# MLP and FFN activations turned by VectorE and through DRAM instead of by TensorE

## The chip, the cores and the metric

One core of one Trainium2 chip. The metric is the device time of one execution in microseconds (us), as a median of several. The core's engines are TensorE (PE; its weight loads are listed apart as PEld), VectorE (DVE), ScalarE (ACT), GpSimd (POOL) and SyncE (SP). Each runs its own instructions in order; they wait for each other by semaphores. Memory transfers are issued by an engine and carried out by 16 DMA engines.

## The reference

256 tokens of width 1024 pass through two blocks in float32. The first has four layers, each a mixer and a squared-ReLU MLP; the second has two layers, each an FFN, a token mixer, another FFN and a gated product:

```
h = squared_relu_mlp(rms_norm(x, g), w1, w2)      # square(relu(x @ w1)) @ w2, 1024 -> 4096 -> 1024
x = x + rms_norm(h, g)
...
x = layer_norm(a * x + 0.5 * (silu(x @ w1) * (x @ w3)) @ w2)      # 1024 -> 2816 -> 1024
x = layer_norm(a * x + token_mixing(x))
x = layer_norm(a * x + 0.5 * swiglu(x))
x = layer_norm(a * x + sigmoid(x @ w_gate) * (p @ w_proj))
```

So there are four MLPs and four FFNs. In both, the inner activations (after relu and square, or after silu and product) are the left operand of the second matrix.

## The kernel before

**Halves and units.** The tokens are cut into two halves of 128 (half 0 and half 1), one Python generator each. A unit is a piece of weights of 128 x 1024. `drive` hands the units out in the order of a plan: half 0 takes a unit, half 1 the same unit some units later (`PACE`: 4 units in these stages). A half's work on one unit is six matmuls of 512 columns, since products are made in three parts (`mm3`): the left operand is split into a rounded high part `t2h` and the rest `t2l`, the weights into `wh` and `whl`; high by high, high by low and low by high are summed.

**Weights.** SP loads a unit into a raw buffer (`raw`, `rawx`: 3 + 2 of them). ScalarE casts it to `wh` or `whx`, VectorE subtracts to get `whl` or `whxl` (`split_unit`). There are 4 + 4 of these pairs. A raw buffer is free again after the subtraction, a pair after half 1's matmuls. In steady running half 1 ends unit v-8 while half 0 works on v-4, so the cast of unit v can begin when half 0 starts unit v-3.

**MLP and FFN.** An MLP has 8 groups of 512 inner columns, an FFN 11 of 256. For group g a half does the first product (`w1(g)`: 4 units) into a PSUM bank `mm`, makes the inner tile (`relu2`, 128x512, or `glu`, 128x256; tokens are the partitions), and later multiplies it by the second matrix (4 or 2 units) into `acc`. For that product the inner index has to lie on the partitions: `tr` turns the tile on TensorE in 128x128 pieces (four or two) into a PSUM bank `tp`, and `split` takes `t2h` and `t2l` from there by ScalarE and VectorE. The order in a half is `w1(0)`, `w1(1)`, product 0, `w1(2)`, product 1, and so on; the last product comes without a first product ahead of it. Product g's second unit is where the split of tile g+1 is asked for.

After an MLP or FFN, a chain on VectorE and GpSimd makes the new `x`, and `x` (or `xn`) is turned on TensorE for the next stage.

**Order.** The program is recorded in this order, and a scheduler then sets each engine's own order by a model of times, so matmuls of the two halves and of neighbouring stages interleave. Small tiles come from two rings (`s1` up to 264 columns, `s2`) whose buffer numbers stand in `RINGS`.

Of the kernel before, what the change touches and what calls it, by code (L numbers as in the profile page):

```python
# [10 lines left out]
F32 = mybir.dt.float32  # L11
# [4 lines left out]
ALU = mybir.AluOpType  # L16
# [8 lines left out]
EXTRA = {"1": (2, 4), "A": (2, 4), "M": (0, 2)}  # L25

RM = (42, 20)
RINGS = {"1": (30, 6), "A": (20, 6), "M": RM}
SIDE_1 = 1.6
H_L = 8.0  # L30
H_P = 9.0
# [19 lines left out]
class Builder:  # L51
    def __init__(s, ctx, tc, io):
        s.ctx, s.tc, s.nc, s.io = ctx, tc, tc.nc, io
        s.pin = tc.keep_in_program_order
        s.kind = None
        eng = s.nc.tensor
        m0, t0 = eng.matmul, eng.transpose
        def mmp(out, a, b, **k):
            r = m0(out, a, b, **k)  # L59
            n = math.prod(b.shape[1:])  # L60
            K = b.shape[0]
            f = b.dtype == F32R
            s.clock += (0.000417 * n if f else 0.001668 * max(n, 0.96 * math.prod(a.shape[1:])) * (0.75 if K == 64 else 0.6 if K == 32 else 1))
            return s.pin(r) if s.kind in PINK else r
        def trp(*a, **k):
            r = t0(*a, **k)  # L66
            s.clock += 0.107
            return s.pin(r) if s.kind in PINK else r
        s.clock = 0.0
        eng.matmul, eng.transpose = mmp, trp  # L70
        pool = lambda name, bufs, **k: ctx.enter_context(tc.tile_pool(name=name, bufs=bufs, **k))
        s.const = pool("const", 1)
        s.raw = pool("raw", RAWP)
        s.wsp = pool("wsp", WHP)
        s.vec = pool("vec", 4)
        s.st = pool("st", 8)
        s.ps = pool("ps", 1, space=PSUM)
        s.turn = False
        s.stack = None
        s.plan, s.width, s.segs = [], {}, []  # L80
        s.rawq, s.whq = ["raw"] * RAWP, ["wh"] * WHP
        s.slot, s.r, s.w, s.sh = {}, {}, {}, {}
        s.loaded = s.split_to = 0
        s.loaded_par = None
        s.pin_ = {}
        s.spaced = False
        s.splits = 0
        s.first_cast = s.first_rin = None
        nc = s.nc
        s.ident = s.const.tile([128, 128], F32, name="ident")  # L90
        make_identity(nc, s.ident)
        s.nhalf = s.const.tile([128, 1], F32, name="nhalf")
        nc.vector.memset(s.nhalf, -0.5)


    def phase(s, kind, what):
# [4 lines left out]
        s.pool = s.stack.enter_context(s.tc.tile_pool(name=f"ph{len(s.slot)}", bufs=1))  # L101
        s.rings = RINGS[kind]
        s.spaced = False
# [236 lines left out]
    def split(s, src):  # L340
        nc = s.nc
        n = src.shape[1]
        hh = s.B2((128, n, 128), "t2h", F32R)
        ll = s.B2((128, n, 128), "t2l", F32R)
        a = nc.scalar.copy(hh, src)  # L345
        b = nc.vector.tensor_tensor(ll, src, hh.bitcast(F32), op=ALU.subtract)  # L346
        if s.splits < 2:
            s.first_split = a.ins, b.ins
        s.splits += 1
        return hh, ll  # L350

    def tr(s, src, n=4):
        tp = s.tpb()
        for j in range(n):
            s.nc.tensor.transpose(tp[:, j, :], src[:, j * 128:(j + 1) * 128], s.ident)
        return tp

    def tr_split(s, src):
        return s.split(s.tr(src))
# [84 lines left out]
    def mlp(s, h, lhs, rin):  # L444
        nc = s.nc
        out = [s.acc(), s.acc()]
        r = {}

        def w1(g):
            mm = s.mmb()  # L450
            for k in range(0, 8, 2):
                W = yield "w1"
                for kk in range(2):
                    s.mm3(lhs, k + kk, W, [(mm, kk * 512, 512, k + kk == 0, k + kk == 7)])
            a = s.B2(name="relu")
            nc.scalar.activation(a, mm, AF.Relu, scale=rin)
            a2 = s.B2(name="relu2")
            nc.vector.tensor_tensor(a2, a, a, op=ALU.mult)
            r[g] = a2

        yield from w1(0)
        for g in range(8):
            if g < 7:
                yield from w1(g + 1)
            at = nxt if g else [s.tr_split(r.pop(g))]
            for k in range(4):
                W = yield "w2"
                if g < 7 and k == 1:
                    nxt = [s.tr_split(r.pop(g + 1))]
                s.mm3(at, k, W, [(out[c], c * 512, 512, g == 0 and k == 0, g == 7 and k == 3) for c in range(2)])  # L470
        return out

# [368 lines left out]
    def ffn(s, h, lhs):  # L841
        nc = s.nc
        out = [s.acc(), s.acc()]
        r = {}

        def w1(g):
            mm = s.mmb()
            for k in range(0, 8, 2):
                W = yield "f1"
                for kk in range(2):  # L850
                    s.mm3(lhs, k + kk, W, [(mm, kk * 512, 512, k + kk == 0, k + kk == 7)])
            a = s.B2((128, 256), "silu")
            nc.scalar.activation(a, mm[:, 0:256], AF.Silu)
            b = s.B2((128, 256), "glu")
            nc.vector.tensor_tensor(b, a, mm[:, 256:512], op=ALU.mult)
            r[g] = b

        yield from w1(0)
        for g in range(11):
            if g < 10:  # L860
                yield from w1(g + 1)
            at = nxt if g else [s.split(s.tr(r.pop(g), 2)[:, 0:2, :])]
            for k in range(2):
                W = yield "f2"
                if g < 10 and k == 1:
                    nxt = [s.split(s.tr(r.pop(g + 1), 2)[:, 0:2, :])]
                s.mm3(at, k, W, [(out[c], c * 512, 512, g == 0 and k == 0, g == 10 and k == 1) for c in range(2)])
        return out

# [993 lines left out]
```

## Time and profile before

| | |
|---|---|
| median of 3 runs | 3048.03 us (3047.71 to 3049.62) |
| profiled execution | 3047.4 us, its span 3045.6 us |
| TensorE's granted clock | 0.991 |
| busy: TensorE, VectorE, ScalarE, GpSimd | 2955.9, 1927.2, 1537.8, 224.1 us |
| SP's DMA queue | 247424 packets, 470.82 MB, 50.5% of 16 engines' span |
| HBM | 494.28 MB read, 1.05 MB written |

The span is the time from the first to the last instruction; 1.8 us of the execution lie around it. In a group's row the text is: line, engine, operation, result tile `<-` operand tiles, shape, count, then busy time in us, mean time of one in ns, idle time before them and who ended it. A row of the timeline has start and length in us; DMA rows have the size and the median time from issue to landing. `SPq` and `POOLq` are the parts of SP and GpSimd that issue.

### The profile page before, as it was taken

The numbers are of one execution on the slowest core, as the hardware profiler recorded it, in microseconds if no ns is written. First come the engines' busy times: TensorE is split into PE (matmuls) and PEld (weight loads), VectorE is DVE, ScalarE is ACT, GpSimd is POOL, SyncE is SP. The second block draws the span as 40 slices with busy tenths as digits, with TensorE's granted clock in tenths as the row PEclk, the third lists the DMA queues.
The fourth block names the chain that finished last, engine by engine and source line by source line (L and its number), as shares of the span: only waits on it lengthen the run. The fifth ranks groups of instructions, "written<-read, shape, count | busy, mean of one in ns | idle before, by whom it ended". The sixth has DMA issues, their size and how long they took to land. (4 is left out here: it accounts for less than half of the span.)

```text
span 3045.6 us, 48487 instructions
## 1 busy us (share of the span) xinstructions
PE 2955.9 (97%) x19034; PEld 2375.1 (78%) x19034; DVE 1927.2 (63%) x3039; ACT 1537.8 (50%) x2358; POOL 224.1 (7%) x352
## 2 busy tenths in 40 slices
PE   8999998999999999999999999999999999999998
PEld 6778876787788778787887877778878788777786
DVE  7565578656755766655557757565665676666656
ACT  4454453545544434544447565444454477653543
POOL 0000024000000000200001100000010001000000
PEclk9999999999999999999999999999999999999999
DMA  7456642566566655665655333466666542344763
GB/s 240 155 181 187 187 152 76 173 186 189 180 192 186 183 163 175 213 186 181 186 156 149 93 105 107 130 212 188 190 199 188 152 132 78 106 119 138 223 186 122
DMA packets 256325, 498.52 MB, mean 164 GB/s; under 512 B 24917, under 2 KB 125473, under 8 KB 256096
## 3 DMA queue, kind: packets, MB, share of 16 engines
q1 hardware_dynamic: 247424, 470.82, 50.5%
q0 software_dynamic: 8096, 22.49, 2.5%
q8 instruction: 150, 2.46, 0.3%
q10 hardware_dynamic: 576, 2.10, 0.2%
q14 instruction: 79, 0.65, 0.1%
HBM read 494.28 MB, written 1.05 MB: 163 GB/s over the span
## 5 line engine op out<-in xcount | busy, mean ns | idle before, releaser
L59 PE MATMUL acc<-wh,t2h 128*128 128x512 f32 (+1 forms) x1512 | 622.8, 413 | 8.9 <-ACT t2h L345 5.5
L59 PE MATMUL acc<-whl,t2h 128*128 128x512 f32 (+1 forms) x1512 | 594.0, 394 | 0.4 <-DVE whl L220 0.4
L220 DVE TENSOR_TENSOR whl<-raw,wh 128x1024 fp32r<-128x1024 f32 (+1 forms) x341 | 412.9, 1212 | 278.0 <-ACT wh L219 274.4
L219 ACT CAST wh<-raw 128x1024 fp32r<-128x1024 f32 (+1 forms) x341 | 355.7, 1044 | 382.9 <-PE acc L59 259.6
L59 PE MATMUL acc<-wh,t2l 128*128 128x512 f32 (+1 forms) x1512 | 509.7, 394 | 2.3 <-DVE t2l L346 2.2
L220 DVE TENSOR_TENSOR whxl<-raw,whx 128x1024 fp32r<-128x1024 f32 x272 | 331.6, 1221 | 207.5 <-ACT whx L219 207.1
L219 ACT CAST whx<-raw 128x1024 fp32r<-128x1024 f32 x272 | 285.0, 1050 | 269.8 <-PE mm L59 133.8
L59 PE MATMUL acc<-whx,t2h 128*128 128x512 f32 x856 | 349.9, 409 | 1.8 <-ACT t2h L345 1.1
L59 PEld LDWEIGHTS acc<-wh,t2h 128*128 128x128 f32 x1512 | 287.3, 190 | 79.1 <-ACT t2h L345 12.9
L59 PEld LDWEIGHTS acc<-wh,t2l 128*128 128x128 f32 x1512 | 285.4, 189 | 66.9 <-DVE t2l L346 5.3
L59 PE MATMUL acc<-whxl,t2h 128*128 128x512 f32 x856 | 337.3, 395 | 0.0
L59 PEld LDWEIGHTS acc<-whl,t2h 128*128 128x128 f32 x1512 | 287.5, 190 | 52.8 <-DVE whl L220 1.8
L59 PE MATMUL mm<-whx,t2h 128*128 128x512 f32 x800 | 313.6, 392 | 1.8 <-ACT whx L219 1.3
L59 PE MATMUL mm<-whx,t2l 128*128 128x512 f32 x800 | 312.2, 390 | 0.7 <-DVE t2l L346 0.7
L59 PE MATMUL mm<-whxl,t2h 128*128 128x512 f32 x800 | 312.0, 390 | 0.8 <-DVE whxl L220 0.8
L59 PE MATMUL acc<-whx,t2l 128*128 128x512 f32 x856 | 285.2, 394 | 0.9 <-DVE t2l L346 0.9
L220 DVE TENSOR_TENSOR whl<-rawx,wh 128x1024 fp32r<-128x1024 f32 x145 | 177.4, 1225 | 141.1 <-ACT wh L219 140.6
L220 DVE TENSOR_TENSOR whxl<-rawx,whx 128x1024 fp32r<-128x1024 f32 x142 | 173.4, 1222 | 124.8 <-ACT whx L219 124.7
L219 ACT CAST wh<-rawx 128x1024 fp32r<-128x1024 f32 x145 | 152.1, 1050 | 152.2 <-PE acc L59 97.1
L219 ACT CAST whx<-rawx 128x1024 fp32r<-128x1024 f32 x142 | 148.5, 1048 | 139.9 <-PE mm L59 94.9
L59 PEld LDWEIGHTS acc<-whx,t2h 128*128 128x128 f32 x856 | 161.5, 189 | 38.9 <-issue 4.8
L59 PEld LDWEIGHTS acc<-whx,t2l 128*128 128x128 f32 x856 | 161.0, 188 | 37.4 <-DVE t2l L346 2.3
(612 smaller groups left out, 4176.0 us busy)
## 6 DMA issues: line engine op xcount, KB each, us to landing
raw<-in_mlp_w SPq DMA_DIRECT2D x153, 512.0 KB, 3.7
raw<-in_w_in SPq DMA_DIRECT2D x128, 512.0 KB, 3.6
raw<-in_ffn_w SPq DMA_DIRECT2D x216, 256.0 KB, 3.1
rawx<-in_mlp_w SPq DMA_DIRECT2D x103, 512.0 KB, 3.7
rawx<-in_ffn_w SPq DMA_DIRECT2D x136, 256.0 KB, 3.1
raw<-in_ret_w_in SPq DMA_DIRECT2D x58, 512.0 KB, 4.3
raw<-in_ffn_w SPq DMA_DIRECT2D x53, 512.0 KB, 3.7
rawx<-in_ret_w_in SPq DMA_DIRECT2D x38, 512.0 KB, 4.3
```

The source lines that it names most:

```text
L59: r = m0(out, a, b, **k)
L219: c = nc.scalar.copy(wh[:, 0:n], r[:, 0:n])
L220: nc.vector.tensor_tensor(wl[:, 0:n], r[:, 0:n], wh[:, 0:n].bitcast(F32), op=ALU.subtract)
```

## The change

A new function `tr_dma` takes the place of TensorE's transposes for the inner tiles of MLP and FFN; all other transposes stay. VectorE turns the tile in 32x32 blocks (`tz`). GpSimd writes it to a DRAM buffer `td` (one DMA, 2 or 1 KB a partition). SP reads it back in four DMAs, one for each 32 of the 128 inner columns of a piece, to that quarter of the partitions of `ty` (128 rows of 512 or 256 bytes each), so that whole 128x128 pieces are turned. `split` then reads `ty` from SBUF in runs of 32 elements instead of `tp` from PSUM. `tr_dma` is called where the tile is made; `split` stays where it was. The ring `s1` of the second block grows from 6 to 12.

```
-RINGS = {"1": (30, 6), "A": (20, 6), "M": RM}
+RINGS = {"1": (30, 6), "A": (20, 12), "M": RM}
...
+        s.dram = pool("dram", 4, space=bass.MemoryType.DRAM)
...
     def split(s, src):
...
-        a = nc.scalar.copy(hh, src)
-        b = nc.vector.tensor_tensor(ll, src, hh.bitcast(F32), op=ALU.subtract)
+        cut = (lambda t: t.rearrange("p c (b j) -> p c b j", j=32)) if len(src.shape) == 4 else (lambda t: t)
+        a = nc.scalar.copy(cut(hh), src)
+        b = nc.vector.tensor_tensor(cut(ll), src, cut(hh.bitcast(F32)), op=ALU.subtract)
...
+    def tr_dma(s, src, n):
+        nc = s.nc
+        z = s.B2((128, 4, n, 32), "tz")
+        nc.vector.transpose(z, src.rearrange("p (c a j) -> p a c j", a=4, j=32))
+        d = s.dram.tile([128, 4, n * 32], F32, tag=f"td{n}", bufs=4, name="td")
+        nc.gpsimd.dma_start(d, z.rearrange("p a c j -> p a (c j)"))
+        y = s.B2((128, 4, n, 32), "ty")
+        for a in range(4):
+            nc.sync.dma_start(y[32 * a:32 * a + 32].rearrange("i b c j -> i b (c j)"),
+                              d.rearrange("(b i) a x -> a i b x", b=4)[a])
+        return y.rearrange("p b c j -> p c b j")
...
-            r[g] = a2
+            r[g] = s.tr_dma(a2, 4)
...
-            at = nxt if g else [s.tr_split(r.pop(g))]
+            at = nxt if g else [s.split(r.pop(g))]
...
-                    nxt = [s.tr_split(r.pop(g + 1))]
+                    nxt = [s.split(r.pop(g + 1))]
...
-            r[g] = b
+            r[g] = s.tr_dma(b, 2)
...
-            at = nxt if g else [s.split(s.tr(r.pop(g), 2)[:, 0:2, :])]
+            at = nxt if g else [s.split(r.pop(g))]
...
-                    nxt = [s.split(s.tr(r.pop(g + 1), 2)[:, 0:2, :])]
+                    nxt = [s.split(r.pop(g + 1))]
```

**ScalarE in the middle of an FFN**, before (numbers tell buffers apart: `silu_12519` becomes the tile that is turned into `tp_12558` and split into `t2h_12561`):

```order
L853 ACTIVATE silu_12519<-mm_12435 128x256
L219 CAST whx_12542<-rawx_12440 128x1024
L219 CAST whx_12572<-rawx_12458 128x1024
L853 ACTIVATE silu_12554<-mm_12474 128x256
L345 CAST t2h_12561<-tp_12558 128x256
L219 CAST whx_12590<-raw_12485 128x1024
L219 CAST wh_12617<-raw_12504 128x1024
L345 CAST t2h_12600<-tp_12597 128x256
```

The same place now (`silu_12559` becomes `ty_12567` and `t2h_12616`):

```order
L869 ACTIVATE silu_12559<-mm_12478 128x256
L220 CAST wh_12591<-raw_12483 128x1024
L220 CAST wh_12627<-raw_12501 128x1024
L869 ACTIVATE silu_12603<-mm_12514 128x256
L220 CAST wh_12645<-rawx_12525 128x1024
L220 CAST whx_12669<-rawx_12544 128x1024
L347 CAST t2h_12616<-ty_12567 128x256
L220 CAST whx_12688<-raw_12576 128x1024
L220 CAST whx_12720<-raw_12595 128x1024
L347 CAST t2h_12652<-ty_12611 128x256
```

The split has moved from two weight casts behind its silu to four.

**SP in the middle of an MLP**, now; before, weight loads alone stand there:

```order
L200 DMA raw_7776<-in_mlp_w1 128x2x512
L370 DMA ty_7709<-td_7707 32x4x128 x4
L200 DMA raw_7808<-in_mlp_w1 128x2x512
L200 DMA rawx_7826<-in_mlp_w2 128x1024
L200 DMA rawx_7848<-in_mlp_w2 128x1024
L200 DMA raw_7866<-in_mlp_w2 128x1024
L370 DMA ty_7792<-td_7790 32x4x128 x4
L200 DMA raw_7898<-in_mlp_w2 128x1024
```

Four reads come after every four weight loads, in the same queue; each four wait for the write of their `td`.

**TensorE at the end of the first FFN**, before (`acc_11668` and `acc_11669` are half 1's; `t2h_13097` is its last tile, `x0_80` the new `x` of half 0, turned for token mixing; half 0's last matmul stands 22 matmuls ahead of those transposes, outside this piece):

```order
L59 MATMUL acc_11669<-whxl_12947,t2h_12967 128x512
L59 MATMUL acc_11668<-whx_12946,t2l_12968 128x512
L59 MATMUL acc_11669<-whx_12946,t2l_12968 128x512
L59 MATMUL acc_11668<-wh_12978,t2h_13097 128x512
L59 MATMUL acc_11668<-whl_12979,t2h_13097 128x512
L59 MATMUL acc_11669<-wh_12978,t2h_13097 128x512
L59 MATMUL acc_11669<-whl_12979,t2h_13097 128x512
L66 MATMUL mm_13124<-ident_73,rwrow_10715 128x94
L66 MATMUL tp_13138<-ident_73,x0_80 128x128 x4
L66 MATMUL mm_13147<-ident_73,x0_80 128x128 x4
L59 MATMUL acc_11668<-wh_12978,t2l_13098 128x512
```

Now (`acc_11817` is half 0's, `acc_11935` and `acc_11936` half 1's, `t2h_13354` its last tile but one, `t2h_13487` its last):

```order
L59 MATMUL acc_11817<-wh_13385,t2l_13390 128x512
L59 MATMUL acc_11936<-whx_13307,t2h_13354 128x512
...
L59 MATMUL acc_11935<-whx_13327,t2l_13355 128x512
L59 MATMUL acc_11936<-whx_13327,t2l_13355 128x512
L66 MATMUL mm_13514<-ident_75,rwrow_10946 128x94
L66 MATMUL tp_13528<-ident_75,x0_82 128x128 x4
L66 MATMUL mm_13537<-ident_75,x0_82 128x128 x4
L59 MATMUL acc_11935<-wh_13365,t2h_13487 128x512
```

Half 0's last matmul (the first row) now stands ten matmuls ahead of the transposes of `x0`, and all of half 1's last product behind them.

## The prediction

> **What bounds the kernel now.** I read the page's first part, the busy time by stretch, the groups by shape, the order of time on TensorE, and last the DMA issues.
>
> ```profile
> span 3045.6 us, 48487 instructions
> PE 2955.9 (97%) x19034; PEld 2375.1 (78%) x19034; DVE 1927.2 (63%) x3039; ACT 1537.8 (50%) x2358; POOL 224.1 (7%) x352
> ```
>
> TensorE works for 97% of the span. The busy times of eight stretches, which hold the four MLPs and the four FFNs, say the same of the place that is changed (the columns after the length are busy time and instructions of each engine):
>
> ```profile
> core 0: us, PE busy (x) PEld busy (x) DVE busy (x) ACT busy (x) POOL busy (x), PEclk, DMA share, GB/s
> 230.00:410.00 180.00, 179.61 (x828) 147.37 (x827) 103.07 (x108) 89.97 (x109) 4.35 (x8) 1.00 0.61 186
> ...
> sum 1454.00, PE 1448.26 PEld 1186.92 DVE 826.50 ACT 689.68 POOL 48.33; mean PE 181.03 PEld 148.37 DVE 103.31 ACT 86.21 POOL 6.04
> ```
>
> The first of the eight stands here with their sum. There TensorE idles for 5.7 us of 1454. VectorE (57%), ScalarE (47%) and GpSimd (3%) have room, and the DMA engines are busy for some 61%. So time is won by taking work from TensorE, and lost where TensorE has to wait for something new.
>
> **What leaves TensorE.** 432 transposes of 128x128:
>
> ```profile
> L66 PE MATMUL tp<-ident,relu 128*128 128x128 f32 x256 | 38.3, 272 | 0.0
> L66 PE MATMUL tp<-ident,glu 128*128 128x128 f32 x176 | 33.4, 271 | 0.0
> ```
>
> Their busy time (71.7 us) overlaps their neighbours, so I price them by how far they push the next matmuls apart. In order of time, four in an MLP and two in an FFN (start, length, instruction):
>
> ```profile
> 240.79 0.39 PE L59 MATMUL mm<-whx,t2l 128*128 128x512 f32 x1
> 241.03 0.60 PE L66 MATMUL tp<-ident,relu 128*128 128x128 f32 x4
> 241.38 0.48 PE L59 MATMUL mm<-wh,t2h 128*128 128x512 f32 x1
> ...
> 242.16 0.40 PE L59 MATMUL mm<-wh,t2h 128*128 128x512 f32 x1
> ...
> 1587.49 0.39 PE L59 MATMUL mm<-wh,t2l 128*128 128x512 f32 x1
> 1587.72 0.38 PE L66 MATMUL tp<-ident,glu 128*128 128x128 f32 x2
> ...
> 1588.42 0.39 PE L59 MATMUL acc<-whx,t2h 128*128 128x512 f32 x1
> 1588.65 0.40 PE L59 MATMUL acc<-whxl,t2h 128*128 128x512 f32 x1
> ```
>
> Undisturbed matmuls start 0.23 us apart (1588.42 to 1588.65). From 240.79 to the fourth matmul after it are 1.37 us instead of 0.92: 0.45 us for four transposes. From 1587.49 to 1588.65 are 1.16: 0.24 us for two. There are 64 and 88 such blocks: 64 x 0.45 + 88 x 0.24 = 28.8 + 21.1 = 50 us, all on the path. Bounds: the time from the first transpose to the next matmul alone (0.35 and 0.14) gives 35 us, the busy time 72. I take 50, since it counts what follows too.
>
> **What comes in.** Each of the 152 tiles now takes this road: ScalarE and VectorE make it as before, VectorE turns it, GpSimd issues its write, SP four reads, and ScalarE and VectorE split it.
>
> ```profile
> L456 ACT ACTIVATE relu<-mm,rin 128x512 f32<-128x512 f32 x64 | 44.2, 690 | 71.4 <-PE mm L59 71.4
> L458 DVE TENSOR_TENSOR relu<-relu 128x512 f32<-128x512 f32 x64 | 44.0, 687 | 33.4 <-ACT relu L456 33.4
> L855 DVE TENSOR_TENSOR glu<-silu,mm 128x256 f32<-128x256 f32 x88 | 36.6, 416 | 31.2 <-ACT silu L853 31.2
> L853 ACT ACTIVATE silu<-mm 128x256 f32<-128x256 f32 x88 | 33.9, 385 | 88.3 <-PE mm L59 88.3
> L1102 DVE STREAM_TRANSPOSE invTT<-invT 128x256 f32<-128x256 f32 x20 | 8.8, 439 | 0.2
> L1102 DVE STREAM_TRANSPOSE invTT<-invT 128x128 f32<-128x128 f32 x20 | 6.2, 311 | 0.6
> L345 ACT CAST t2h<-tp 128x256 fp32r<-128x256 f32 x88 | 32.5, 370 | 29.9 <-PE acc L59 26.4 <-PE tp L66 3.5
> L345 ACT CAST t2h<-hoT 128x512 fp32r<-128x512 f32 x8 | 4.8, 625 | 0.0
> ```
>
> The block turn has these two rows: 0.44 us for 256 columns, 1.0 ns more per column, so 0.70 for 512. That is 64 x 0.70 + 88 x 0.44 = 83 us more on VectorE, or 63% of the stages instead of 57%: hidden. Splitting out of SBUF costs ScalarE 0.63 instead of 0.59 a tile: hidden. The transfers (issue to landing last):
>
> ```profile
> v<-in_norm_g POOLq DMA_DIRECT2D x32, 256.0 KB, 4.6
> p<-in_p POOLq DMA_DIRECT2D x4, 128.0 KB, 3.3
> raw<-in_w_in SPq DMA_DIRECT2D x8, 16.0 KB, 2.5
> raw<-in_mlp_w SPq DMA_DIRECT2D x153, 512.0 KB, 3.7
> out<-x ACTq DMA_DIRECT2D x2, 512.0 KB, 2.7
> 1520.10 0.89 SPq L199 DMA_DIRECT2D rawx<-in_ffn_w  x2
> ```
>
> For the writes I take GpSimd's rows of the same size (loads, the nearest): 4.6 us in an MLP, 3.3 in an FFN; between 2.7 (the one write to DRAM, from another queue) and twice that. A read of 64 or 32 KB lies near the 16 KB row: 2.6 us, between 2.5 and 3.7. SP issues every 0.45 us (two in 0.89), so the fourth read starts 1.3 us after the first. From the last matmul to the first half of the split, in an FFN: 0.39 + 0.42 + 0.44 + 3.3 + 1.3 + 2.6 + 0.37 = 8.8 us; in an MLP: 0.69 + 0.69 + 0.70 + 4.6 + 1.3 + 2.6 + 0.63 = 11.2. At the two visits to ScalarE and VectorE another cast or subtraction may stand ahead; for that I add half of one twice, 1.1 us: **9.9 and 12.3 us**.
>
> [...]
>
> **In the middle of a stage all of it is hidden.** In the new order 78 matmuls (FFN) and 102 (MLP) stand on TensorE between a tile's last matmul and the first that uses its split: 17.8 and 23.2 us, against 9.9 and 12.3. What else waits meanwhile? On ScalarE the split stands four weight casts, about 11 us, behind its silu: it can hold up the next cast by a little. On SP the reads wait for the write, and weight loads are queued behind them.
>
> ```profile
> 300.17 0.33 SPq L199 DMA_DIRECT2D rawx<-in_mlp_w  x1
> 311.89 1.05 ACT L219 CAST wh<-rawx 128x1024 fp32r<-128x1024 f32 x1 [0.67 <-PE acc L59]
> SPq L199 <- DVE whl L220: 1164.6, 381, 24.7
> ```
>
> Weight buffers are used in rotation, so the load of 300.17 belongs to the cast of 311.89: landed after 3.7 us, it lay 8.0 us. The cast itself began when TensorE freed its buffer, three units ahead of its use; a unit is 12 matmuls or 2.7 us, so after the cast (1.05) and VectorE's subtraction (1.2) some 5.9 us are left. SP's four issues (1.8 us) fit into its 1164.6 us of waiting for VectorE. A hold-up below 8 us on SP or 5.9 on ScalarE costs nothing.
>
> **At the end of a stage it is not.** Half 1's last tile has less ahead of it. MLP: 48 matmuls, 10.9 us, against 12.3: 1.4 us, four times, 5.6. First and third FFN, where token mixing follows: half 0's last product now stands behind half 1's last first-layer unit, and only ten matmuls (2.3 us) are left between it and the next stage's transposes of `x`. Before:
>
> ```profile
> 1594.35 0.62 PE L59 MATMUL acc<-wh,t2l 128*128 128x512 f32 x2
> 1594.78 1.29 DVE L885 SCALAR_TENSOR_TENSOR z<-acc,x 128x512 f32<-128x512 f32 x2 [2.30 <-PE acc L59]
> 1599.13 1.41 DVE L891 SCALAR_TENSOR_TENSOR x<-z,rstd,v 128x512 f32<-128x512 f32 x2
> 1600.15 0.60 PE L66 MATMUL tp<-ident,x 128*128 128x128 f32 x4
> ```
>
> Half 0's last matmul starts at 1594.58 (0.23 after the row's first), and the first half of `x` is ready at 1599.87 (1599.13 and one 0.74): 5.3 us. With ten matmuls between, the transposes would come to their turn 11 x 0.23 = 2.5 us after that last matmul's start: 2.8 us of waiting arise. In it half 1's road goes on: 24 matmuls (5.5), the 2.8 and eight transposes (0.9) cover 9.2 of 9.9: 0.7 more. 2 x 3.5 = 7.0. In the other two FFNs 24 matmuls of the next product come ahead of `x` (25 x 0.23 = 5.7 against 5.3) and 48 ahead of the last tile (10.9 against 9.9): nothing. Half 0's own last tile has 44 matmuls, 10.0 us, in the worst place: nothing.
>
> **Sum** against the profiled execution (3047.4 us outside, 0.6 below the median of 3048.0): 3047.4 - 50 + 5.6 + 7.0 = **3010 us**.
>
> **Rivals.** (a) The roads are no longer than their cover at the MLPs' ends too, or the waits at the ends are filled: 3047.4 - 50 + 5.8 = 3003, with no waits at all 2997. For it: the 2.7 us write. Against: GpSimd's own rows.
> (b) A longer write. Writes of twice 4.6 and 3.3 us add 4.6 to each MLP's end, 3.3 to the ends of the first and third FFN, and 13.2 - 10.9 = 2.3 to those of the other two: 3010 + 18.4 + 6.6 + 4.6 = 3040; the middle (17.8 against 13.2) still holds. For it: DMA engines already busy for 61%, and loads of 4.6 us on GpSimd's queue where SP's twice as large ones take 3.7. [...]
> (c) Slower: the reads stuck on SP. If write and reads take long enough that a road outlasts 17.8 us, every FFN group stalls, and SP holds weight loads as long. That needs 8 us more than I count, 15 instead of 7.2 for write and reads. At a road of 20 us, 2.2 us in each of 40 FFN groups: 3010 + 88 = 3098; 3047 is passed near 18.8. Against it: write and read would both have to take 6.8 us (6.8 + 1.3 + 6.8 = 15), in every group, and the slowest row above is 4.6.
> (d) No change: a gain eaten at the ends, in the range between (b) and (c).
>
> **How the numbers follow.** My forecast (3004 to 3018) 0.45, with 0.05 more for the weaker form of (b); (a) 0.22; (b), 3018 to 3040, 0.17; (d) 0.04; (c) 0.07. The range leaves out the lowest part of (a), (c), (d) and the top of (b): 2996 to 3032. Two tenths of a per cent (6 us) is about what can be told here: faster 0.88, the same 0.04, slower 0.08.
>
> **What the profile after would show.** No `tp<-ident,relu` or `glu`; TensorE's busy time down by about 50 us; block turns of 0.70 and 0.44 us; writes landing in 3.3 to 4.6 us; no wait of TensorE for weights in the middle; waits for `t2h` at the MLPs' ends (1 to 2 us) and for `x` after the first and third FFN (3 us). I am wrong if TensorE waits for `wh` or `whx`, or for `t2h` in every group, or if weight casts wait for loads.

## The result, and the profile after

The changed kernel takes 3097.07 us (median of 4 runs, 3093.24 to 3101.65), the kernel before 3047.87. The ratio is 1.0162 [1.0144, 1.018]: 1.6% slower, where 1.2% faster was forecast. The profiled execution took 3099.7 us, its span 3097.9. The page after, its span and busy times:

```profile
span 3097.9 us, 49526 instructions
PE 2940.1 (95%) x18602; PEld 2351.3 (76%) x18602; DVE 1997.6 (64%) x3191; ACT 1534.9 (50%) x2358; POOL 306.0 (10%) x504
```

432 transposes are gone from TensorE (19034 less 18602), but its busy time fell by 15.8 us instead of 50, and its idle time (span less busy) rose from 89.7 to 157.8. The parts that were added are of the predicted size. The DMA issues after (last column: us to landing) and the turns (mean ns behind the comma):

```profile
td<-tz POOLq DMA_DIRECT2D x64, 256.0 KB, 4.3
ty<-td SPq DMA_DIRECT2D x256, 64.0 KB, 2.0
td<-tz POOLq DMA_DIRECT2D x88, 128.0 KB, 3.3
ty<-td SPq DMA_DIRECT2D x352, 32.0 KB, 2.0
raw<-in_mlp_w SPq DMA_DIRECT2D x153, 512.0 KB, 4.5
L365 DVE STREAM_TRANSPOSE tz<-relu 128x512 f32<-128x512 f32 x64 | 45.5, 711 | 2.0
L365 DVE STREAM_TRANSPOSE tz<-glu 128x256 f32<-128x256 f32 x88 | 39.2, 445 | 2.9
```

Write, read and turn are as forecast or shorter. Weight loads land 0.8 us later than before (4.5 against 3.7). The middles of the stages are hidden as predicted. Two stretches after, one in the first MLP and one in the first FFN (second column PE busy, then the number of matmuls; 1.00 is the granted clock):

```profile
300.00:388.00 88.00, 88.00 (x390) 72.88 (x389) 55.05 (x57) 43.02 (x49) 4.32 (x8) 1.00 0.74 242
1490.00:1602.00 112.00, 112.00 (x496) 92.74 (x495) 65.98 (x82) 51.99 (x68) 7.31 (x14) 1.00 0.75 228
```

TensorE never waits in them. An MLP group takes 21.7 us instead of 22.7, an FFN group 16.3 instead of 16.9 (from one tile's last matmul to the same half's next): the gain is there. What took it away shows in the list of waits (total us, times, longest):

```profile
ACT t2h L347 <- DMA ty<-td: 127.3, 63, 8.6
...
PE acc L59 <- ACT t2h L347: 59.6, 26, 7.2
...
ACT whx L220 <- DMA raw<-in_mlp_w: 18.5, 8, 4.6
...
SPq L370 <- DMA td<-tz: 440.5, 136, 8.7
```

Before, TensorE's line was:

```profile
PE acc L59 <- ACT t2h L345: 6.6, 9, 2.2
```

The rows like the third, ScalarE's casts waiting for the loads of MLP and FFN weights, add up to 65.7 us, against 11.7 before: one of the prediction's own signs of being wrong.

By stage, measured at a stage's first matmul and at the first use of its last tile, the delay against before grew by 3.1, 2.8, 0.4 and 11.1 us in the four MLPs and by 0, 6.6, 12.5 and 5.2 in the four FFNs, where each should have shrunk by some 7 (MLP) or 5 (FFN); the rest of the 52 us arose between them. The long waits stand at the starts and the ends of stages, and from the middle of the fourth MLP and of the third FFN on.

### The profile page after: what moved, and what is told of

Read it like the earlier page. It is cut to its first block, busy times and chain, and to the rows that moved or that the text cites. A ratio compares the mean times of both kernels' runs of the same rounds, so it can differ in the third digit from the quotient of the medians.

```text
span 3097.9 us, 49526 instructions
## 1 busy us (share of the span) xinstructions
PE 2940.1 (95%) x18602; PEld 2351.3 (76%) x18602; DVE 1997.6 (64%) x3191; ACT 1534.9 (50%) x2358; POOL 306.0 (10%) x504
## 5 line engine op out<-in xcount | busy, mean ns | idle before, releaser
L367 POOL DMA_DIRECT2D td<-tz x152 | 82.4, 542 | 1241.2 <-DVE tz L365 1218.9
```

The source lines that it names most:

```text
L367: nc.gpsimd.dma_start(d, z.rearrange("p a c j -> p a (c j)"))
```

## The experiments

Five theories came out of the traces. **E**: the roads of the middle tiles are free, and the loss arises at the edges, from the first tiles' and the last tile's roads. **H**: on ScalarE, which works in order, the next tile's relu stands behind a split that waits for its transfers. **S**: SP stands at the four reads until their write has landed, and weight loads queue behind them. **G**: GpSimd issues the writes behind the token mixer's parameter loads. **D**: the added traffic slows other transfers. A sixth suspicion, that the gain was never there, came first. All ratios are to the kernel before, run beside them on the same chip; kernels of different groups are compared by these ratios.

### What the transposes cost, and what the transfers cost without the wait

`no_turn` is the kernel before with the transposes out (in the FFN alike); the next three add the change's parts to it, with nothing using what they bring:

```diff
-                    nxt = [s.tr_split(r.pop(g + 1))]
+                    nxt = [s.split(r.pop(g + 1).rearrange("p (c j) -> p c j", j=128))]   # no_turn
...
+            nc.vector.transpose(z, a2.rearrange("p (c a j) -> p a c j", a=4, j=32))       # turn_alone
+            s.tr_dma(a2, 4)                                                               # ghost
-            nc.sync.dma_start(y[32 * a:32 * a + 32]...
+            nc.gpsimd.dma_start(y[32 * a:32 * a + 32]...                                  # ghost_pool
```

> The kernel before with the 432 transposes left out and nothing in their place: the split reads relu and glu as they stand, so the products are computed from tiles that were not turned. It shows what the transposes cost TensorE. By the spacing of matmuls: 50 us, 2997 us; by the bounds of the prediction 35 to 72, 2976 to 3012. If the gain is less than 35 us, the prediction's gain was the step that failed.

> ghost without its write and reads: VectorE's block turns alone (83 us of work whose result is not used; the products come from tiles that were not turned). ghost lost 49 us against no_turn, in the first microseconds of the MLPs waiting for a weight load that SP issued behind four waiting reads, and elsewhere. If the transfers did that, here no_turn's time returns: 3001 within 6. If VectorE's turns did it, 3030 to 3050.

> All turns, writes and reads of the changed kernel are made, but nothing uses what they bring: the split reads relu and glu as they stand (products of tiles that were not turned), at once, as in no_turn. It has the load on VectorE, GpSimd, SP and the DMA engines without the wait for the road. If the loss comes from waiting for the road (theory E: edges): as no_turn, 3001 within 6. Rival S or D (weight loads held on SP, or slowed by the added transfers): above 3020, in the extreme near 3080.

> ghost with the four reads issued by GpSimd, behind their write, and no longer by SP; nothing waits for them. Theory S (SP stands at the reads until the write has landed, and the weight loads queue behind them): most of the 49 us come back, 3001 to 3015. Theory D (the transfers slow the weight loads, whoever issues them): it stays near 3050.

`ghost_late` moves `ghost`'s reads alone (a new `tr_read`, called at the third weight unit behind the tile, at the second for a last one):

```diff
+                if k == (1 if g == 6 else 2) and g + 1 in d:
+                    s.tr_read(*d.pop(g + 1))
```

> ghost with the four reads of a tile later in SP's order, where their write has landed: some three weight units (8 us) behind it, in a stage's last tile two. Same transfers, same queues, nothing waits for them. Theory S (SP standing at the reads is the cost of ghost): no_turn's time, 3001 to 3010. Theory D (the transfers themselves): what ghost_pool left, 3020 to 3030, or more.

| kernel | us | ratio |
|---|---|---|
| no_turn | 3001.14 | 0.9841 [0.9813, 0.9869] |
| turn_alone | 3006.13 | 0.9847 [0.9816, 0.9877] |
| ghost | 3049.62 | 0.9987 [0.9968, 1.0006] |
| ghost_pool | 3025.19 | 0.99 [0.9873, 0.9928] |
| ghost_late | 3012.10 | 0.9871 [0.9845, 0.9897] |

The gain is real: 0.0159 x 3048 = 48 us, where the prediction had 50. VectorE's turns are free (0.9847 with them, 0.9841 without). But transfers that nobody waits for ate nearly all of it (from `no_turn` to `ghost` 0.0146 x 3048 = 45 us). TensorE's order was not held fixed in this: at the stage borders the scheduler set it otherwise in `ghost` than in `no_turn`, and otherwise again in `turn_alone` and `ghost_late`. How the transfers cost time is seen in `ghost`'s first MLP (timeline of SP, then of ScalarE and TensorE; in brackets the idle time before and who ended it):

```profile
258.92 1.87 SPq L370 DMA_DIRECT2D ty<-td  x4
260.89 2.03 SPq L200 DMA_DIRECT2D rawx<-in_mlp_w  x2
...
269.08 1.04 ACT L220 CAST whx<-rawx 128x1024 fp32r<-128x1024 f32 x1 [8.93 <-DMA rawx<-in_mlp_w]
...
271.13 0.50 PE L59 MATMUL acc<-wh,t2h 128*128 128x512 f32 x1 [3.99 <-ACT wh L220]
```

The weight loads of 260.89 were issued behind the four reads, which had waited for a write issued at 253.12; ScalarE sat 8.93 us for the second of them, and TensorE 3.99. Moving the reads later in SP's order gave 35 of the 45 us back (0.9987 to 0.9871), moving them to another queue 27 (`ghost_pool`, 10 us above its range under S). So S is shown for these transfers, though how much of the 35 us lies in the other order on TensorE was not separated. `ghost_late` is above `no_turn` by 9 us, with intervals that overlap; D is that or nothing.

### ScalarE's and GpSimd's queues

`late_split` asks for the split later; `early_mix` moves the parameter loads; `late_early` does both:

```diff
                 W = yield "w1"
+                if k == 2 and g > 1:
+                    at[g - 1] = [s.split(r.pop(g - 1))]
...
-                if g < 7 and k == 1:
-                    nxt = [s.split(r.pop(g + 1))]
...
-                if i == max(stop - 36, start) and stop < n and s.kind != "M" and end == stop:
+                if i == max(stop - (100 if s.kind == "1" else 72), start) and stop < n and s.kind != "M":
```

> Only the place of the split in the program changes: it is asked for when its product is near (MLP: at the second weight unit of the next first layer, FFN: at the third; the first and the last tile: at their product's first unit), so that on ScalarE and VectorE the other half's relu or silu stands ahead of it. Theory H (the split waits for its transfers at the head of ScalarE's queue, and the next tile's relu behind it starts 5 to 8 us late, so the last road of an MLP is 17 us instead of 12): relu starts within 1.7 us of its matmul again, the waits at the ends of the first three MLPs shrink from 5.5-7.2 us to about 1.5, the small ones at the stage starts go; GpSimd's parameter loads still disturb the fourth MLP and the third FFN. About 3060 us, 3050 to 3070. Rival D (the transfers themselves are long, by contention): 3097 within 5. Rival S (SP holds weight loads while its reads wait for the write): 3097 within 5, the reads stay where they are.

> Only the token mixer's parameter loads (some 20 DMAs that GpSimd issues over 20 us in the middle of the fourth MLP and of the third FFN) move ahead of these stages, to where no tile is written. Theory G (the writes of the tiles queue behind them on GpSimd): the fourth MLP loses some 3 us instead of 11 against before, the third FFN some 6 instead of 12: about 3082 us, 3075 to 3088. If GpSimd's queue is not the cause there: 3097 within 5.

> Both moves at once. Theories H and G together: only the ends remain that the prediction counted (MLP ends 1.4 us each, token mixing's start after the first and third FFN), and the clock with them: 3020 to 3045 us. If H alone holds, as late_split; if neither, 3097.

| kernel | us | ratio |
|---|---|---|
| late_split | 3077.83 | 1.0085 [1.0062, 1.0107] |
| early_mix | 3080.00 | 1.0096 [1.0069, 1.0123] |
| late_early | 3078.21 | 1.0088 [1.0061, 1.0116] |

Each takes 20 to 23 us off the change, and both together no more. `early_mix` came in its range; `late_split` missed its own by 8 us, and `late_early` came out as "H alone". The two moves overlap in the fourth MLP: measured as above, it loses 11.1 us in the change, 0.5 in `early_mix`, and in `late_split`, where the parameter loads stay, it gains 1.8. A split that is asked for later hides a late write too. H in the changed kernel's trace, ScalarE in the middle of the first MLP:

```profile
305.02 0.62 ACT L347 CAST t2h<-ty 128x512 fp32r<-128x512 f32 x1 [0.73 <-DMA ty<-td]
305.55 0.68 ACT L472 ACTIVATE relu<-mm,rin 128x512 f32<-128x512 f32 x1
...
315.92 0.62 ACT L347 CAST t2h<-ty 128x512 fp32r<-128x512 f32 x1 [0.74 <-DMA ty<-td]
316.44 0.69 ACT L472 ACTIVATE relu<-mm,rin 128x512 f32<-128x512 f32 x1
...
326.92 0.62 ACT L347 CAST t2h<-ty 128x512 fp32r<-128x512 f32 x1 [0.87 <-DMA ty<-td]
327.44 0.69 ACT L472 ACTIVATE relu<-mm,rin 128x512 f32<-128x512 f32 x1
```

Read it as a chain: a split waits for its transfer, the other half's relu comes right behind it, and that tile's road (relu at 305.55, its split at 315.92, 10.4 us) ends at the next split. Two links a group are 21.9 us, just TensorE's 21.7. So it costs nothing here, but a delay from the start is never made good: relus start 5 to 8 us late to the end of the stage, where the road has 17 to 19 us from its matmul and not 12. `late_early` at the same place:

```profile
310.29 0.69 ACT L474 ACTIVATE relu<-mm,rin 128x512 f32<-128x512 f32 x1 [0.31 <-PE mm L59]
315.32 0.62 ACT L347 CAST t2h<-ty 128x512 fp32r<-128x512 f32 x1
```

The relu waits for its matmul alone, the split for nothing. The gain fell short at the ends of the first three MLPs, because the scheduler now set two of half 0's eight turns of `xn` 24 instructions earlier on TensorE, ahead of half 1's last product:

```profile
404.96 0.66 PE L66 MATMUL tp<-ident,xn 128*128 128x128 f32 x2 [4.98 <-DVE xn L440]
```

And at the starts of three FFNs TensorE now waited 10.9 us for a `glu`, where the changed kernel waits 1.6. That is S: here SP stood at reads whose write had been issued at 2027.68, the weight loads behind them came late, and so did ScalarE's cast, the silu behind it and the `glu` (`late_early`, second FFN: SP, ScalarE, TensorE):

```profile
2034.09 1.75 SPq L370 DMA_DIRECT2D ty<-td  x4
2035.95 0.90 SPq L200 DMA_DIRECT2D raw<-in_ffn_w  x2
...
2040.20 1.05 ACT L220 CAST whx<-raw 128x1024 fp32r<-128x1024 f32 x1 [3.95 <-DMA raw<-in_ffn_w]
...
2044.55 0.54 PE L59 MATMUL mm<-wh,t2h 128*128 128x512 f32 x1 [3.60 <-DVE glu L874]
```

G in the changed kernel, GpSimd in the fourth MLP:

```profile
1326.34 0.54 POOL L367 DMA_DIRECT2D td<-tz  x1 [10.97 <-DVE tz L365]
1326.87 0.54 POOL L948 DMA_DIRECT2D cm<-in_c_mix  x1
...
1346.32 0.54 POOL L973 DMA_DIRECT2D gab<-in_gdn_a_log  x1
1346.85 0.54 POOL L367 DMA_DIRECT2D td<-tz  x1
```

For 20 us it issues nothing but parameter loads; the second tile here was turned 5.5 us before its write was issued. In `early_mix` that is gone, and its time is the expected one.

Two more runs moved the reads to GpSimd's queue (the `ghost_pool` edit), in the changed kernel and in `late_early`:

> The changed kernel with only this edit: the reads on GpSimd's queue. By S some of the loss goes (3060 to 3085), by H most stays, since ScalarE still stands at the split; GpSimd issues 2 us for the four reads and stands at its own write, so a second tile's write comes later, and at the ends of stages, where the road is on the path, a loss of 1 to 2 us each is possible. If S is nothing: 3097 to 3115.

> late_early (split late, parameter loads early) with the reads on GpSimd's queue. If H, G and S are the three causes, what is left is the ends: 3040 to 3055. If S is nothing: 3078 or more.

`reads_pool` took 3281.55 us, 1.0776 [1.0715, 1.0838]; `late_early_pool` 3104.31, 1.0163 [1.0136, 1.0191]. The first lies far outside every range given for it. The second lies where it was expected if S were nothing, but it can't decide on S, since on that queue its 64 KB reads land after 4.7 us, where the changed kernel's land after 2.0 from SP's. The pair is the sharpest test of H. The landing in `reads_pool`:

```profile
ty<-td POOLq DMA_DIRECT2D x256, 64.0 KB, 5.5
```

With it ScalarE's chain has longer links than TensorE's pace (`reads_pool`, first MLP):

```profile
303.25 0.62 ACT L347 CAST t2h<-ty 128x512 fp32r<-128x512 f32 x1 [10.01 <-DMA ty<-td]
303.77 0.68 ACT L472 ACTIVATE relu<-mm,rin 128x512 f32<-128x512 f32 x1
...
317.00 0.62 ACT L347 CAST t2h<-ty 128x512 fp32r<-128x512 f32 x1 [6.91 <-DMA ty<-td]
317.52 0.69 ACT L472 ACTIVATE relu<-mm,rin 128x512 f32<-128x512 f32 x1
...
331.98 0.62 ACT L347 CAST t2h<-ty 128x512 fp32r<-128x512 f32 x1 [9.99 <-DMA ty<-td]
```

Two links are 28.7 us (303.25 to 331.98), and the whole MLP runs at that pace. The same edit costs 0.0614 (187 us) where the relu stands behind the split and 0.0075 (23 us) where it does not.

### Edges and middle

These kernels choose by tile number who turns a tile. `middle` is `late_early` with the road for tiles 2 to 6 of an MLP and 2 to 9 of an FFN; `not_last` for all but the last; `middle_as_was`, `only_last` and `only_first` are the change with its split and parameter loads where they were:

```diff
-            r[g] = s.tr_dma(a2, 4)
+            r[g] = s.tr_dma(a2, 4) if g in range(2, 7) else a2      # only_last: (7,); only_first: (0, 1)
```

> late_early, with TensorE's transposes back for the first two tiles and the last of each MLP, and the first two and the last of each FFN; tiles 2 to 6 of 8 and 2 to 9 of 11 keep the road. Theory E (all loss arises at the starts and ends of the stages): 40 blocks of 0.45 us and 64 of 0.24 are saved, 33 us: 3015, 3010 to 3020. If roads cost in the middle too: above 3030.

> The changed kernel with the split and the parameter loads left where the change had them, and only the first two and the last tiles of each stage back on TensorE. If the order on ScalarE hurts by itself, through the whole stage, well above middle (3030 and more); if it only kept a delay that the start had made, little above it: middle plus the parameter loads' 5 to 15 us.

> late_early, with TensorE's transposes back for the last tile of each stage alone. It parts the ends from the starts. The waits for xn and for the split at the ends go (5 and 1 us in each of three MLPs, 3.4 in the fourth, 3 to 5 in each FFN, some 30 us, and slow matmuls behind each), for 5.5 us of transposes that come back: about 3040 if the rest is lost at the starts, 3078 if the ends cost nothing.

> The kernel before, with the road for the last tile of each MLP and FFN alone (16 tiles, as the change builds it; ScalarE's order upstream is that of before). The prediction's term for the ends, by itself: 5.5 us less on TensorE and 12.6 us of waits, 3055. If the ends cost far more than that (waits of 2 us and more, each followed by 3 us at half clock, 1.7 us lost): 3065 to 3085.

> The kernel before, with the road for the first two tiles of each MLP and FFN alone (32 tiles). The prediction counted nothing here: 11 us less on TensorE, 3037. If weight loads held on SP and ScalarE's queue cost at the starts what middle against not_last says (13 us and the 11): 3055 to 3068.

| kernel | us | ratio |
|---|---|---|
| middle | 3018.25 | 0.9875 [0.9842, 0.9909] |
| middle_as_was | 3021.14 | 0.9888 [0.9859, 0.9917] |
| not_last | 3031.14 | 0.9917 [0.9887, 0.9947] |
| only_last | 3068.39 | 1.0059 [1.004, 1.0078] |
| only_first | 3079.07 | 1.0104 [1.0068, 1.014] |

E holds for the middle. `middle` saves 38 us (33 expected), and TensorE's line of waits is before's own:

```profile
PE acc L59 <- ACT t2h L347: 6.6, 9, 2.2
```

`middle_as_was` is level with it: without the edges neither the order on ScalarE nor the parameter loads cost anything that can be told. The edges by themselves make the kernel slower than before: `only_last` by 18 us, so with the 5.5 that its 16 blocks save the last tiles cost 23; `only_first` by 32, so with its 11 the first two cost 43. (`only_first` lies 11 us above its higher range, `not_last` 9 below its lower value.) In `only_last` TensorE's waits for the split:

```profile
PE acc L59 <- ACT t2h L347: 13.3, 11, 2.6
```

6.7 us more than before, none of it at an MLP's end, where with the relu on time the road takes 10 to 11 us. By the delay against before, each MLP's last product even comes 0.8 to 1.0 us earlier relative to the stage's start, as the tile's transposes are gone, and all of the loss lies at the four FFN ends: some 4.6, 5.3, 7.0 and 5.3 us. At the first and third the transposes of `x` wait 2.0 and 3.1 us, as the prediction had it. At the second and fourth the two longest waits of this line, 2.60 us each, are not for a tile of the road: they are for the split of the turned `x`, which on ScalarE stands behind a weight cast that waits for half 1's last product, now set later on TensorE. (The profile is of an execution 13 us above its median. 12 us of its delay arise in another stage, with a wait of 9.3 us for GpSimd that the kernels before and after do not show.) The starts, ScalarE in `only_first`'s first MLP:

```profile
249.92 1.05 ACT L220 CAST whx<-rawx 128x1024 fp32r<-128x1024 f32 x1 [1.33 <-DMA rawx<-in_mlp_w]
250.87 0.68 ACT L472 ACTIVATE relu<-mm,rin 128x512 f32<-128x512 f32 x1
...
263.13 0.62 ACT L347 CAST t2h<-ty 128x512 fp32r<-128x512 f32 x1 [5.61 <-DMA ty<-td]
268.32 1.05 ACT L220 CAST whx<-rawx 128x1024 fp32r<-128x1024 f32 x1 [4.58 <-DMA rawx<-in_mlp_w]
```

At 250.87 half 1's first relu starts, 7.1 us behind its matmul (243.8): a split and two casts that waited for late loads stood ahead. Its split comes at 263.13 and TensorE waits; the next cast waits for a load 4.58 us more.

Three kernels then took the reads later in SP's order, as `ghost_late` does: `late_all` in `late_early`, `not_last_late` in `not_last`, and `one_to_six_late`, which leaves the first tile to TensorE as well.

> late_early with the reads late in SP's order too; all tiles take the road. Under S the starts are relieved, and what is left is the waits at the ends: 3050 to 3065. If SP costs nothing beside the ends: 3078; above that, if the later reads lengthen the last roads.

> not_last with the reads later in SP's order (some 8 us behind their write): every tile but a stage's last takes the road. not_last lost some 24 us at the starts. If SP's standing at the reads is their cause there too, most comes back: 3008 to 3018, level with middle or better. If not: 3031 as not_last.

> The same, and the first tile of each stage goes back to TensorE too (tiles 1 to 6 of 8, 1 to 9 of 11 take the road). By the saving alone (48 blocks of 0.45 us, 72 of 0.24, 39 us): 3009, 3006 to 3016. If the second tile's road is still on the path: above 3018, middle's time.

`late_all`: 3068.27 us, 1.0058 [1.0038, 1.0077]. `not_last_late`: 3022.11, 0.9906 [0.9872, 0.994]. `one_to_six_late`: 3011.26, 0.9851 [0.9824, 0.9878]. In the traces S goes: the casts' waits for MLP and FFN weights fall from 61.6 us (`late_early`) to 34.1 (`late_all`) and from 67.7 (`not_last`) to 30.5 (`not_last_late`), and TensorE's waits for `glu`, 10.9 and 11.0 us, are gone. So S acts where the reads are used, too. What it is worth in time is not shown: by the ratios the first two are 9 and 3 us under the kernels they come from, with overlapping intervals; `late_all` is 3 us above its range under S, `not_last_late` between its two. `not_last_late` still has four waits of 1.8 to 3.6 us for the first tiles' splits, and with the first tile on TensorE they go. So at the starts the first tile's road is itself on the path. `one_to_six_late` beats both kernels, by 45 us the one before (39 expected from its saving).

## Why the prediction was wrong, step by step

**TensorE's gain, 50 us: right** (48).

**The road, 9.9 and 12.3 us: right in its parts.** Where nothing stands ahead it is 9.2 to 10.9 us in the first FFN, as forecast, and 10 to 11 at the MLPs' ends in `only_last`, a little shorter. Rival (b), longer writes, fell, and the weaker form of it that has 0.05 of the chances too: the writes landed in 4.3 and 3.3 us, against 4.6 and 3.3 forecast.

**The middle hidden: right**, for TensorE; `middle`, 38 us faster than before, is the proof.

**"It can hold up the next cast by a little": the step that failed.** The prediction asked what stands behind the split on ScalarE and saw weight casts. In the MLPs the other half's relu stands there, so one tile's wait becomes the next one's delay. SP's cushion of 8 us failed likewise at the starts of stages, where loads are not yet ahead: casts waited 65.7 us for loads in the changed kernel, 11.7 before, and 11.5 in `middle`, whose first tiles have no reads.

**The starts of stages: a term left out.** The sum had nothing there; `only_first` measured 43 us. In the changed kernel the road of a stage's first tile took 11.4 to 21.2 us.

**The ends, 5.6 + 7.0: mis-sized.** On their own the MLPs' ends cost nothing (forecast 1.4 us of waiting each), and the FFNs' ends cost all of the 23 us, the second and fourth, which the sum had at nothing, 5.3 each: it looked at the tile's road and not at what a later last product does to the split of `x`. In the full change the first three MLP ends waited 5.5 to 7.2 us, because H's delay arrived there. The wait for `x` after the first and third FFN, forecast 2.8 us, was 2.6 and 5.5.

**The clock after a wait: a term left out.** The changed kernel and `no_turn` issue the same 18602 instructions on TensorE:

```profile
span 2997.3 us, 47632 instructions
PE 2906.9 (97%) x18602; PEld 2336.3 (78%) x18602; DVE 1928.9 (64%) x3039; ACT 1537.1 (51%) x2358; POOL 225.0 (8%) x352
```

Of the 100.6 us between the spans 33.2 are busy time (2940.1 against 2906.9), the same work done more slowly, and 67.4 are waiting. The granted clock of the whole span, 0.980 against 0.990, withholds some 31 us more, about the 33. After the longest wait (end of the first MLP):

```profile
399.06 0.61 PE L59 MATMUL acc<-wh,t2l 128*128 128x512 f32 x2
406.83 0.80 PE L59 MATMUL acc<-whx,t2h 128*128 128x512 f32 x1 [7.16 <-ACT t2h L347]
407.43 0.63 PE L59 MATMUL acc<-whxl,t2h 128*128 128x512 f32 x1
407.85 0.63 PE L59 MATMUL acc<-whx,t2h 128*128 128x512 f32 x1
```

Matmuls start 0.42 us apart and not 0.23, for 3.4 us; the granted clock of that stretch (after the busy times) is half:

```profile
406.80:410.00 3.20, 3.17 (x8) 2.52 (x9) 2.10 (x4) 1.43 (x5) 0.17 (x1) 0.50 0.22 77
```

So this wait cost 7.2 + 1.7 us.

**The rivals.** (c), "the reads stuck on SP", gave 3098 and was the nearest in time, but by another way: it wanted 20 us roads in every FFN group, and those are hidden. Its mechanism was half right, at the edges, where SP's stand is seen (10.9 us of waits for `glu` in `late_early`). (Rival (a) adds 5.8 where its terms make 2 x 2.8 = 5.6; nothing rests on it.) That the change could lose had 0.08; the sign was wrong with it.

**What stays open.** Gain 48, first tiles 43, last tiles 23: that makes 18 us slower, and the change is 49 slower. The other 31 arise only where the whole row of tiles takes the road: by the traces they are the delays that H carries from the starts to the ends and that G adds. `late_split` and `early_mix` each give 20 back and together no more, in the fourth MLP because they mend the same loss; elsewhere how they overlap was not settled. What S is worth in time in the changed kernel stays open too.

## What to carry to other kernels

When an operation is replaced by a road through memory, price it at the first and the last use of each stage, where the cover is thin (here, on their own, the first two tiles of the stages cost 43 us and the last 23); keep the old way there and use the road in the middle (`middle` saves 38). Look at what stands behind the waiting instruction on each in-order engine and queue: if it is the start of the next road, waits chain, and the sum of the links must stay under the bottleneck's pace (two links of 21.9 us, level with TensorE's 21.7, cost nothing in the middle of the first MLP; 28.7 in `reads_pool` set the whole MLP's pace). In the changed kernel 21 of TensorE's 22 waits of 2 us or more cost more than their length.

## What the hardware showed that was not expected

Of the changed kernel's 22 waits of TensorE of 2 us or more (the one at the kernel's start left out), 21 have the granted clock at 0.50 behind them, from some time in the wait or within 1.9 us of its end, for 3.4 us or a multiple. Of the 41 waits of 0.5 to 2 us, 3 do. Where matmuls run through 3.4 us of it, it costs half of that, 1.7. After the wait of 2.61 us that ended at 583.46:

```profile
584.30:587.70 3.40, 3.40 (x10) 2.63 (x9) 2.90 (x4) 0.65 (x2) 0.16 (x1) 0.50 1.01 306
```

The same 64 KB reads landed after 2.0 us from SP's queue, and from GpSimd's, where each four follow GpSimd's own write, after 5.5 us in `reads_pool` and 4.7 in `ghost_pool` and `late_early_pool`.
